# Two-block kernel: router work placed between projection matmuls, rows gathered in transposed halves, expert and feed-forward matmuls reordered

## The chip, the cores and the metric

One core of one Trainium2 chip runs the whole program, one launch. The metric is the device time in microseconds; the kernel before was timed three times, 1625.5, 1627.11 and 1628.01 us, median 1627.11.

## What is computed

256 tokens of 1024 values pass a first block and then a second. In the first block a norm, a projection, attention of the stick-breaking kind and a recurrent state mixer are followed by an output projection that is added to the stream. Then comes the mixture of experts that the change touches:

```python
xn = rmsnorm(h)
grp_prob = softmax(xn @ w_grp + b_grp);  g_idx = top-1 of 4 groups
sel = (xn @ w_exp + b_exp) of the 8 experts of that group;  top-2 of softmax(sel)
combine = group value * expert value / sum of the two expert values
for e in range(32):
    y = y + combine[:, e:e+1] * ((silu(xn @ w_gate[e]) * (xn @ w_up[e])) @ w_down[e])
h = rmsnorm(h + y) * final_norm_g
```

An expert is 1024 to 256 and back to 1024. The second block has two layers of feed-forward (1024 to 2816 and back), a mixer, and feed-forward again; each feed-forward is `x + 0.5 * (silu(x @ w_gate) * (x @ w_up)) @ w_down`.

## The kernel before

**Words.** P is 128, the tokens are two tiles of 128 (j = 0, 1), the 1024 columns two halves (n = 0, 1) of 512. `K.mx` is a PSUM pool of two buffers of two banks, `K.acc` one of four buffers of one bank. Weights of the second block are split into a high part wh (ScalarE, line 277) and a rest wl (VectorE, line 258), and the stream likewise, so that a product takes three matmuls. Most small operations go through wrappers (class InOrder, its call on line 48) that keep the order of the program on their engine; the profile gives them all line 48. What is not written with the wrappers (`K.ordered = False` with `nc.tensor`, line 246) may be reordered by the framework's scheduler.

**Front's end** (from `out_sb`, about lines 907 to 954). The output projection runs over eight weight units f; its last four (f = 4 to 7, list `us`) are held for both token tiles. With `K.ordered` set, the first tile's projection is finished and added to x, its factor is computed, then the second tile's projection runs: column half 0 over four units, the first tile's transposes (`turn`, `turned`), column half 1, then the first tile's router logits.

**Moe.run.** 96 loads of 1 MB (gate, up and down of 32 experts, in quads q of four: 4 gate, 4 up, 4 down) go on SP's queue into 22 ring slots. The slots alias tiles of the front, so that a load waits until the front's last reader of that place is done; the 16th load (gate of expert 7) lies on held output-projection weights, the next ones on the first tile's transposed rows and further weights. From the 23rd load on (`load_next(4)`, three times a quad) a load waits for the matmuls that read the slot's last content. Of the last load (down of expert 31) the two column halves are issued as two transfers.

At its start the second tile is added, transposed and given its logits; `select(j)` (twelve VectorE steps) picks group and experts of a tile, a product with a triangular matrix ranks the tokens of an expert, and one-hot matrices `OH[j]` of 32 slots an expert come out of it. `weave` alternates the steps of two such lists. `with_x(j, n)` starts the accumulators `py[j, n]` with x itself. Then, for each quad:

- `up(q, 0)`, `up(q, 1)`: gate and up of the quad's 4 x 32 slot rows, four experts side by side on TensorE (tile 128*32);
- `gather(q+1, j)`: the next quad's rows, one-hot times x; copied to SBUF by ScalarE and VectorE (`gathered`), transposed with a column step of 8, scaled and copied (`rows_T`, tiles XG0 and XG1);
- `act`: Silu on ScalarE, a product on VectorE, two transposes, a copy to hT;
- `down`: hT times the four experts' down weights, for n = 0 and then n = 1;
- `back(q, y, n)`: y is split into yh (ScalarE) and yl (VectorE) and added to `py[j, n]` through the transposed one-hot.

In quad 0 the slot weights and the rest of the `with_x` come in too. `all_tokens` is a branch for experts with more than 32 tokens.

**The tail** (from `V, S = K.V, K.S`). For each j and n: `square` (ScalarE, sum of squares of py), `gained` (VectorE, py times a gain into x) and `square_x` (ScalarE, squares of that). Their order is written out by hand, with quad 7's second `back` between. From the sums `e0` (twelve small VectorE steps) makes the factor of the second block's first norm, and `xn` is the first tile that TensorE transposes for the second block.

**Feed-forward** (from line 1728, `for i in range(1, FF // 256)`). For each column block i four accumulators (gate and up, two halves b each) collect over four weight units. X is stored as high part and rest side by side, so a wh matmul has 512 columns and a wl matmul 256. In a unit all eight wh matmuls of the four accumulators come first, then all eight wl matmuls. Blocks with even i use the mx pool, with odd i the acc pool; the down stage ("dn") uses 512 columns throughout.

## Time and profile before

| what | value |
|---|---|
| median of three runs | 1627.11 us |
| profiled execution: its own time | 1625.12 us |
| profiled execution: span of the core | 1623.4 us |
| granted clock, mean | 0.981 |
| PE busy | 1549.9 us, 95% of the span |
| DVE, ACT busy | 64%, 51% |
| moved by DMA | 331 MB, mean 204 GB/s |

The profile shows one execution. Times of its rows count from the start of the span; the engines are PE (TensorE), PEld (its weight loads), DVE (VectorE), ACT (ScalarE), POOL (GpSimd) and SP (the engine whose queue issues the loads). A timeline row is `start, length, engine, line, operation, out<-in, shape, xcount`, and in brackets the idle time of the engine ahead of it and what ended that; equal instructions in a row are one row. The ends of matmuls are modelled and overlap their successors: the pitch of matmuls is read from starts. PSUM tiles all bear the name of their pool (mx, acc).

### The profile page before, as it was taken

What the parts mean: (1) busy time and instruction counts of PE and PEld (TensorE: products, weight loads), DVE (VectorE), ACT (ScalarE), POOL (GpSimd) and SP (SyncE); (2) the same over time, 40 slices, a digit from 0 to 9 for tenths busy, and PEclk for the clock granted to TensorE, in tenths of its full rate; (3) what the DMA queues carried; (4) which work ended last, traced back from release to release, by engine and by line L of the source; (5) the groups of instructions that cost most, each with busy time, mean ns of one, the idle gap of its engine ahead of it and who ended that gap; (6) DMA issues with size and microseconds to landing.
All of it is one profiled execution on the core that took longest, in us unless ns stands there. A gap on an engine that the chain in (4) does not pass through costs nothing.

```text
span 1623.4 us, 25106 instructions
## 1 busy us (share of the span) xinstructions
PE 1549.9 (95%) x9734; PEld 1283.6 (79%) x9734; DVE 1036.6 (64%) x1916; ACT 828.3 (51%) x1408; POOL 43.5 (3%) x134
## 2 busy tenths in 40 slices
PE   7999998887799999999999999999999999999998
PEld 6989874343378888889878888888888989778887
DVE  7866551111377656868986665666648779876653
ACT  6633421111356544668645554456546687455643
POOL 4000000000100000000000000000000000000000
PEclk9999998999999999999999999999999999999999
DMA  6431599999956555553456665656566434556653
GB/s 209 136 102 66 202 369 388 421 420 420 374 182 194 182 194 176 181 163 104 156 182 195 185 196 183 202 182 185 176 203 203 157 118 151 173 157 188 197 178 111
DMA packets 195644, 331.29 MB, mean 204 GB/s; under 512 B 11972, under 2 KB 150674, under 8 KB 183362
## 3 DMA queue, kind: packets, MB, share of 16 engines
q1 hardware_dynamic: 186208, 315.19, 56.4%
q0 software_dynamic: 4528, 13.41, 2.5%
q8 instruction: 77, 1.26, 0.3%
q10 hardware_dynamic: 4786, 1.05, 0.3%
q14 instruction: 45, 0.37, 0.1%
HBM read 328.25 MB, written 1.38 MB: 203 GB/s over the span
## 4 chain that ended last, share of the span: by engine, by line
PE 70%; DMA 6%; DVE 4%; ACT 2%; issue 1%; SPq 0%; ACTq 0%; DVEq 0%
PE acc L246 39%; PE mx L246 19%; PE acc L48 7%; PE mx L48 4%; DMA mw<-in_exp_w_down 2%; DMA mw<-in_exp_w_up 1%; DMA mw<-in_exp_w_gate 1%; DVE wl L258 1%; DVE wl L48 1%; PE mx L1969 0%; DMA wr<-in_w_in 0%; ACT wh L277 0%; PE mx L1993 0%; DMA wr<-in_ffn_w_up 0%; DVE ul L258 0%
## 5 line engine op out<-in xcount | busy, mean ns | idle before, releaser
L258 DVE TENSOR_TENSOR wl<-wr,wh 128x1024 fp32r<-128x1024 f32 x358 | 436.7, 1224 | 269.8 <-ACT wh L277 267.3
L277 ACT ACTIVATE wh<-wr 128x1024 fp32r<-128x1024 f32 x358 | 377.9, 1058 | 363.3 <-PE acc L246 249.5
L246 PE MATMUL acc<-X,wh 128*128 128x256 f32 (+1 forms) x1664 | 357.1, 329 | 0.0
L246 PEld LDWEIGHTS acc<-X,wh 128*128 128x128 f32 x1664 | 277.2, 191 | 25.4 <-issue 4.2
L246 PE MATMUL acc<-X,wl 128*128 128x256 f32 x1152 | 237.2, 284 | 0.0
L246 PEld LDWEIGHTS acc<-X,wl 128*128 128x128 f32 x1152 | 186.3, 191 | 6.9
L246 PE MATMUL mx<-X,wh 128*128 128x512 f32 x640 | 161.9, 393 | 0.0
L246 PEld LDWEIGHTS mx<-X,wh 128*128 128x128 f32 x640 | 114.5, 189 | 19.9
L246 PE MATMUL acc<-wh,hh 128*128 128x512 f32 x288 | 112.1, 389 | 0.0
L246 PE MATMUL acc<-wl,hh 128*128 128x512 f32 x288 | 112.1, 389 | 0.0
L246 PE MATMUL acc<-wh,hl 128*128 128x512 f32 x288 | 112.0, 389 | 0.0
L246 PEld LDWEIGHTS mx<-X,wl 128*128 128x128 f32 x640 | 88.3, 190 | 7.0
L246 PE MATMUL mx<-X,wl 128*128 128x256 f32 x640 | 90.5, 282 | 0.0
L48 PE MATMUL mx<-mw,XG 128*32 128x256 f32 x1024 | 64.6, 396 | 9.3 <-DMA mw<-in_exp_w_up 5.9
L48 PEld LDWEIGHTS mx<-mw,XG 128*32 128x32 f32 x1024 | 34.2, 114 | 37.9 <-issue 9.2
L246 PEld LDWEIGHTS acc<-wh,hl 128*128 128x128 f32 x288 | 54.1, 188 | 11.3
L246 PEld LDWEIGHTS acc<-wh,hh 128*128 128x128 f32 x288 | 54.1, 188 | 11.2
L246 PEld LDWEIGHTS acc<-wl,hh 128*128 128x128 f32 x288 | 54.1, 188 | 11.0
L246 PE MATMUL acc<-wh,m 128*128 128x512 f32 x192 | 61.4, 394 | 0.0
L48 DVE COPY xr<-mx 128x512 f32<-128x512 f32 x8 | 5.5, 691 | 74.1 <-ACT xr L48 74.1
L246 PE MATMUL acc<-xh,wh 128*128 128x256 f32 x176 | 50.3, 286 | 0.0
L246 PE MATMUL acc<-xh,wl 128*128 128x256 f32 x176 | 49.9, 283 | 0.0
(641 smaller groups left out, 2537.4 us busy)
## 6 DMA issues: line engine op xcount, KB each, us to landing
wr<-in_w_in SPq DMA_DIRECT2D x44, 1024.0 KB, 5.4
wr<-in_ffn_w_gate SPq DMA_DIRECT2D x88, 512.0 KB, 4.0
wr<-in_ffn_w_up SPq DMA_DIRECT2D x88, 512.0 KB, 5.1
wr<-in_ffn_w_down SPq DMA_DIRECT2D x40, 1024.0 KB, 5.0
mw<-in_exp_w_gate SPq DMA_DIRECT2D x32, 1024.0 KB, 14.8
mw<-in_exp_w_up SPq DMA_DIRECT2D x32, 1024.0 KB, 16.7
mw<-in_exp_w_down SPq DMA_DIRECT2D x31, 1024.0 KB, 17.6
wr<-in_w_out SPq DMA_DIRECT2D x20, 1024.0 KB, 5.0
```

Of the source, the lines that this page charges most:

```text
L48: return lambda *a, **k: self.tc.keep_in_program_order(f(*a, **k))
L246: self.engines()[2].matmul(out, l, r, start=start, stop=stop, skip_group_check=share)
L258: i = self.K.engines()[0].tensor_sub(l, v, h)
L277: self.K.engines()[1].activation(h, v[:, q:q + c], AF.Copy)
```

## The change

The order of the front's end: half of the second tile's projection is moved behind the first tile's transposes, and the first tile's logits, the second tile's first add and its first transposes ahead of the last units. `gather` reads x with a column step of 8, so that the gathered rows come out in the order in which the transposes want them; copying and transposing go by halves with tiles of their own (xr0, xr1). The start of Moe.run runs the first tile's selection ahead of the second tile's logits, and the second tile's selection in one piece between the two gathers. In a quad the activation's first two steps go ahead of the next gather, and the first half's result is copied while the second half's matmuls run. In quad 7 the second half is split: experts 28 to 30 with the others, expert 31 behind the first half's `back` and the squares. The tail's squares are in a new order. In the feed-forward units each accumulator gets its two wh and then its two wl matmuls before the next accumulator's turn.

```diff
@@ -940,18 +940,24 @@
             out_mm(u, f, 0, n, False, True)
             router.add(x, 0, n, acs[0, n], acs[0, n])
         run(router.factor(0))
-        for n in range(2):
-            if n:
-                for h in range(2):
-                    router.turn(x, 0, h)
-                for h in range(2):
-                    router.turned(0, h, xT[h])
-            for f, u in us:
+
+        def last(n, fu):
+            for f, u in fu:
                 out_mm(u, f, 1, n, False, f == 7)
-        for n in range(2):
-            router.logits(0, n, xT[n])
+        last(0, us[:2])
+        for h in range(2):
+            router.turn(x, 0, h)
+        for h in range(2):
+            router.turned(0, h, xT[h])
+        last(0, us[2:])
+        last(1, us[:2])
+        for h in range(2):
+            router.logits(0, h, xT[h])
+        router.rest = [acs[1, n] for n in range(2)]
+        router.add(x, 1, 0, acs[1, 0], acs[1, 0])
+        router.turn(x, 1, 0)
+        last(1, us[2:])
         K.ordered = False
-        router.rest = [acs[1, n] for n in range(2)]
 
 
 NRING = 22
@@ -1113,34 +1119,40 @@
             return [lambda: K.V.tensor_add(rank[:, j], negm[:, j], pr[:, j]), lambda: place(j, 0, 4)]
 
 
-        XG, pg, xr = [None, None], [None], [None]
+        XG, pg, xr = [None, None], [None], [None, None]
 
         def gather(q, j):
 
             if j == 0:
-                pg[0] = K.mx.tile([P, 2, 512], F32, name="mx")
+                pg[0] = K.mx.tile([P, 2, 4, P], F32, name="mx")
             for n in range(2):
-                K.mm(pg[0][:, n], OH[j][:, 4 * q:4 * q + 4].rearrange("p e c -> p (e c)"), x[:, j, n * 512:(n + 1) * 512],
-                     j == 0, j == 1, share=True)
-
-        def gathered():
-            xr[0] = wk.tile([P, 2, 512], F32, name="xr")
+                K.mm(pg[0][:, n], OH[j][:, 4 * q:4 * q + 4].rearrange("p e c -> p (e c)"),
+                     x[:, j].rearrange("p (f k) -> p k f", k=KD)[:, 4 * n:4 * n + 4], j == 0, j == 1, share=True)
+
+        def gathered(n):
             V, S, _ = K.engines()
-            S.activation(xr[0][:, 0], pg[0][:, 0], AF.Copy)
-            V.tensor_copy(xr[0][:, 1], pg[0][:, 1])
-
-        def rows_T():
-
-            pt = K.mx.tile([P, KD, P], F32, name="mx")
-            r = xr[0].rearrange("p n f -> p (n f)")
+            xr[n] = wk.tile([P, 4, P], F32, name=f"xr{n}")
+            if n:
+                V.tensor_copy(xr[n], pg[0][:, n])
+            else:
+                S.activation(xr[n], pg[0][:, n], AF.Copy)
+
+        pt_ = [None]
+
+        def rows_T(n):
+
+            if n == 0:
+                pt_[0] = K.mx.tile([P, KD, P], F32, name="mx")
+            pt = pt_[0][:, 4 * n:4 * n + 4]
             V, S, T_ = K.engines()
-            for k in range(KD):
-                T_.transpose(pt[:, k], r[:, k::KD], K.ident)
-            for b in range(2):
-                XG[b] = wk.tile([P, 4, P], F32, name=f"XG{b}")
-            V.tensor_mul(XG[0], pt[:, 0:4], gp[:, 0:4, None].to_broadcast([P, 4, P]))
             for k in range(4):
-                S.activation(XG[1][:, k], pt[:, 4 + k], AF.Copy, scale=gp[:, 4 + k:5 + k])
+                T_.transpose(pt[:, k], xr[n][:, k], K.ident)
+            XG[n] = wk.tile([P, 4, P], F32, name=f"XG{n}")
+            if n == 0:
+                V.tensor_mul(XG[0], pt, gp[:, 0:4, None].to_broadcast([P, 4, P]))
+            else:
+                for k in range(4):
+                    S.activation(XG[1][:, k], pt[:, k], AF.Copy, scale=gp[:, 4 + k:5 + k])
         OHT = [None]
 
         def slots_T(q):
@@ -1222,7 +1234,7 @@
                         for j in range(2):
                             K.mm(a[j][:, 0:512], xT[j][k // 4][:, k % 4], g, k == 0, k == KD - 1)
                     for j in range(2):
-                        hT = self.act(wk, a[j], ce[:, j], self.r[j])
+                        _, hT = self.act(wk, a[j], ce[:, j], self.r[j])
                         for n in range(2):
                             for k in range(2):
                                 d = piece(wd[bass.ds(e, 1)].rearrange("o (p k) f -> p (o k) f", k=2)[:, k, n * 512:(n + 1) * 512])
@@ -1236,16 +1248,11 @@
                     K.mm(a[32 * i:32 * i + 32, 256 * hf:256 * hf + 256], XG[k // 4][:, k % 4, 32 * i:32 * i + 32],
                          W["gu", 4 * q + i, hf][:, k], k + hf == 0, k == KD - 1, share=True)
 
-        def down(q, hT):
-            ys = []
-            for n in range(2):
-                y = K.mx.tile([P, 512], F32, name="mx")
-                for k in range(2):
-                    for i in range(4):
-                        K.mm(y[32 * i:32 * i + 32], hT[:, k, 32 * i:32 * i + 32],
-                             W["d", 4 * q + i, 0][:, k, n * 512:(n + 1) * 512], k == 0, k == 1, share=True)
-                ys.append(y)
-            return ys
+        def down_mm(q, hT, y, n, experts):
+            for k in range(2):
+                for i in experts:
+                    K.mm(y[n][32 * i:32 * i + 32], hT[:, k, 32 * i:32 * i + 32],
+                         W["d", 4 * q + i, 0][:, k, n * 512:(n + 1) * 512], k == 0, k == 1, share=True)
 
         def spare(name, slot, dt=F32):
 
@@ -1258,61 +1265,61 @@
             py[j, n] = K.acc.tile([P, 512], F32, name="acc")
             K.mm(py[j, n], K.ident, x[:, j, n * 512:(n + 1) * 512], True, False)
 
-        def back(q, ys, n):
+        yp = {}
+
+        def out_rows(q, y, n):
+
             if q == 7 and n:
                 t = spare("yr", 12, F32R)
-                yh, yl = t[:, 0:512], t[:, 512:1024]
+                yp[n] = t[:, 0:512], t[:, 512:1024]
             else:
-                yh, yl = [wk.tile([P, 512], F32R, name=t) for t in ("yh", "yl")]
-            K.engines()[1].activation(yh, ys[n], AF.Copy)
-            K.engines()[0].tensor_sub(yl, ys[n], yh)
-            for y in (yh, yl):
-                for j in range(2):
-                    K.mm(py[j, n], OHT[0][:, q % 2, j * P:(j + 1) * P], y, False, q == 7 and y is yl)
+                yp[n] = [wk.tile([P, 512], F32R, name=t) for t in ("yh", "yl")]
+            V, S, _ = K.engines()
+            S.activation(yp[n][0], y[n], AF.Copy)
+            V.tensor_sub(yp[n][1], y[n], yp[n][0])
+
+        def back(q, n):
+            yh, yl = yp[n]
+            for j, y in [(0, yh), (0, yl), (1, yh), (1, yl)] if q == 7 else [(0, yh), (1, yh), (0, yl), (1, yl)]:
+                K.mm(py[j, n], OHT[0][:, q % 2, j * P:(j + 1) * P], y, False, q == 7 and y is yl)
 
         K.ordered = True
         xT = [wk.tile([P, 4, P], F32, name="xTm", tag=t) for t in ("XG1", "yh")]
         OH[0] = K.xp.tile([P, NE, CAP], F32, name="OH0", tag="grow")
         OH[1] = (B.c if B else wk).tile([P, NE, CAP], F32, name="OH1", tag="big")
         s0, s1 = select(0), select(1)
-        for n in range(2):
-            self.add(x, 1, n, self.rest[n], self.rest[n])
-        for n in range(2):
-            self.turn(x, 1, n)
-            self.turned(1, n, xT[n])
-        for n in range(2):
-            self.logits(1, n, xT[n])
+        run(s0[:8])
+        self.turned(1, 0, xT[0])
+        self.logits(1, 0, xT[0])
+        self.add(x, 1, 1, self.rest[1], self.rest[1])
+        self.turn(x, 1, 1)
+        self.turned(1, 1, xT[1])
+        run(s0[8:])
         f1 = self.factor(1)
-        run(f1[:4])
-        weave(f1[4:], s0[:6])
-        for n in range(2):
-            with_x(0, n)
-        weave(s0[6:], s1[:6])
         K.mm(pr[:, 0], lt, mask[:, 0])
         K.mm(pr[:, 1], K.ones, mask[:, 0], stop=False, share=True)
-        with_x(1, 0)
-        run(s1[6:8])
-        weave(s1[8:10], ranks(0))
-        run(s1[10:])
+        run(f1[:3])
+        weave(f1[3:5], ranks(0))
+        run(f1[5:])
+        self.logits(1, 1, xT[1])
+        with_x(0, 0)
+        gather(0, 0)
+        run(s1)
         K.mm(pr[:, 1], lt, mask[:, 1], start=False, share=True)
-        gather(0, 0)
         run(ranks(1))
         gather(0, 1)
-        gathered()
-        rows_T()
+        for n in range(2):
+            gathered(n)
+            rows_T(n)
         for j in range(2):
             place(j, 4, NE)
-
-        def rows(q):
-            for j in range(2):
-                gather(q, j)
-            gathered()
 
         for q in range(NE // 4):
             if q == 2:
                 all_tokens(nmax)
             if q == 2:
-                rows_T()
+                for n in range(2):
+                    rows_T(n)
             a = K.mx.tile([P, 1024], F32, name="mx")
             up(a, q, 0)
             load_next(4)
@@ -1327,24 +1334,40 @@
                 slot_weights(0, 1)
             if q % 2 == 0:
                 slots_T(q)
-            if q != 7:
-                rows(q + 1)
             if q == 6 and B:
                 par = B.params(Carve(K.xp.tile([P, D], F32, name="par", tag="grow")))
                 next(par)
-            hT = self.act(wk, a, ws[:, q:q + 1], ws[:, 8 + q:9 + q])
-            if q not in (1, 7):
-                rows_T()
+            act = self.act(wk, a, ws[:, q:q + 1], ws[:, 8 + q:9 + q])
+            next(act)
+            if q != 7:
+                gather(q + 1, 0)
+            hT = next(act)
+            if q != 7:
+                gather(q + 1, 1)
+                for n in range(2):
+                    gathered(n)
+            if q == 0:
+                with_x(0, 1)
+                with_x(1, 0)
             if q == 7 and B:
                 next(par, None)
-            y = down(q, hT)
+            y = [K.mx.tile([P, 512], F32, name="mx") for _ in range(2)]
+            down_mm(q, hT, y, 0, range(4))
+            out_rows(q, y, 0)
+
+            down_mm(q, hT, y, 1, range(3 if q == 7 else 4))
             load_next(4)
+            if q not in (1, 7):
+                for n in range(2):
+                    rows_T(n)
+            back(q, 0)
             if q == 0:
                 slot_weights(1, 8)
                 nmax = beyond()
                 with_x(1, 1)
-            for n in range(1 if q == 7 else 2):
-                back(q, y, n)
+            if q != 7:
+                out_rows(q, y, 1)
+                back(q, 1)
 
         K.ordered = False
 
@@ -1376,19 +1399,19 @@
         def gained(j, n):
             V.tensor_mul(x[:, j, half[n]], py[j, n], fg[:, half[n]])
 
-        gained(0, 0)
-        back(7, y, 1)
-        square(1, 0)
-        square(0, 0)
-        gained(1, 0)
-        gained(0, 1)
-        square_x(0, 0)
-        square(0, 1)
-        gained(1, 1)
-        square_x(0, 1)
-        square(1, 1)
-        square_x(1, 0)
-        square_x(1, 1)
+        for j in range(2):
+            square(j, 0)
+            gained(j, 0)
+            square_x(j, 0)
+        K.ordered = True
+        down_mm(7, hT, y, 1, [3])
+        out_rows(7, y, 1)
+        back(7, 1)
+        K.ordered = False
+        for j in range(2):
+            square(j, 1)
+            gained(j, 1)
+            square_x(j, 1)
         run(e0)
         steps, ra = K.rsqrt_steps(K.sm, a1, [P, 2], 1.0, 0.0, "fr", True)
         return [f[1] for f in fs], ra, e1, steps
@@ -1400,10 +1423,11 @@
         V, S, T_ = K.engines()
         S.activation(sg, a[:, 0:256], AF.Silu, scale=r)
         V.scalar_tensor_tensor(sg, a[:, 256:512], w, sg, op0=OP.mult, op1=OP.mult)
+        yield
         for k in range(2):
             T_.transpose(a[:, 512 + k * P:512 + (k + 1) * P], sg[:, k::2], K.ident)
         S.activation(hT, a[:, 512:768].rearrange("p (k t) -> p k t", k=2), AF.Copy)
-        return hT
+        yield hT
 
 
 NZ, NXBC, NDT = 0, 1024, 2560
@@ -1728,13 +1752,13 @@
         for i in range(1, FF // 256):
             ac = sums(i)
             for wh, wl, k0, m in self.units(("gu", i), 0, KD):
-                bs = [(ac[b][s], slice(s * 256 + b * P, s * 256 + (b + 1) * P)) for b in range(2) for s in range(2)]
-                for a, c in bs:
-                    for k in range(m):
-                        K.mm(a, wh[:, k, c], X[:, k0 + k], k0 + k == 0, False, share=True)
-                for a, c in bs:
-                    for k in range(m):
-                        K.mm(a[:, 0], wl[:, k, c], X[:, k0 + k, 0], False, k0 + k == KD - 1, share=True)
+                for b in range(2):
+                    for s in range(2):
+                        a, c = ac[b][s], slice(s * 256 + b * P, s * 256 + (b + 1) * P)
+                        for k in range(m):
+                            K.mm(a, wh[:, k, c], X[:, k0 + k], k0 + k == 0, False, share=True)
+                        for k in range(m):
+                            K.mm(a[:, 0], wl[:, k, c], X[:, k0 + k, 0], False, k0 + k == KD - 1, share=True)
             if i == 1:
                 pt = K.mx.tile([P, 2, T], F32, name="mx")
                 for j in range(2):
```

## Rows read from the trace of the kernel before

**Rows 1.** The page's 40 equal slices (40.6 us each): the DMA share.
```profile
DMA  6431599999956555553456665656566434556653
```

**Rows 2.** Windows: length, busy PE, PEld, DVE, ACT, POOL, clock, DMA share, GB/s.
```profile
222.00:230.00 8.00, 7.75 (x55) 6.36 (x53) 4.85 (x31) 1.95 (x6) 0.00 (x0) 1.00 0.89 331
242.00:250.00 8.00, 7.31 (x83) 4.03 (x72) 0.77 (x5) 0.60 (x1) 0.00 (x0) 1.00 0.87 324
272.00:280.00 8.00, 8.00 (x124) 4.28 (x117) 0.00 (x0) 0.00 (x0) 0.00 (x0) 1.00 0.82 312
340.00:350.00 10.00, 9.31 (x137) 5.16 (x136) 0.00 (x0) 0.60 (x1) 0.00 (x0) 1.00 1.02 419
470.00:620.00 150.00, 150.00 (x806) 129.77 (x805) 95.85 (x139) 81.81 (x140) 0.00 (x0) 1.00 0.59 190
```

**Rows 3.** Chain of waits, middle of the expert stage: start, us, what.
```profile
333.51 19.82 DMA mw<-in_exp_w_gate
```

**Rows 4.** Timeline of SP's queue: the sixteenth load's issue.
```profile
222.50 0.33 SPq L1046 DMA_DIRECT2D mw<-in_exp_w_gate  x1
```

**Rows 5.** Timeline of TensorE, head of the expert stage: start, us, what.
```profile
222.98 1.87 PE L48 MATMUL acc<-wrt,xT 128*128 128x36 f32 x16
224.68 1.07 PE L48 MATMUL mx<-ident,x 128*128 128x128 f32 x8
231.35 3.68 PE L48 MATMUL mx<-x,OH 128*128 128x512 f32 x8
238.38 1.93 PE L48 MATMUL mx<-mw,XG 128*32 128x256 f32 x32 [0.79 <-DVE XG L48]
```

**Rows 6.** Tile views of xr and x by form: ns min/median/max.
```profile
L48 PEld LDWEIGHTS mx<-ident,xr x64: 186/193/230, 236.4 to 407.4; 128*128 128x128 f32 x64
L48 PEld LDWEIGHTS mx<-ident,x x16: 138/140/225, 219.1 to 225.4; 128*128 128x128 f32 x16
L48 PE MATMUL mx<-x,OH x24: 592/592/697, 231.3 to 281.5; 128*128 128x512 f32 x24
```

**Rows 7.** Timeline of TensorE, quad 0.
```profile
247.22 3.70 PE L48 MATMUL mx<-x,OH 128*128 128x512 f32 x8 [0.69 <-ACT OHT L1153]
253.97 0.54 PE L48 MATMUL mx<-ident,msg 128*128 128x128 f32 x2 [3.06 <-DVE msg L48]
```

**Rows 8.** Timelines of TensorE, ScalarE and VectorE, tail of the expert stage.
```profile
436.65 3.62 PE L48 MATMUL mx<-mw,mhT 128*32 128x512 f32 x26 [0.32 <-DMA mw<-in_exp_w_down]
440.31 0.60 ACT L1267 ACTIVATE yr<-mx 128x512 fp32r<-128x512 f32 x1 [1.06 <-PE mx L48]
442.32 0.60 ACT L48 ACTIVATE fsq<-acc 128x512 f32<-128x512 f32 x1 [0.21 <-DVE x L48]
441.55 2.49 DVE L48 TENSOR_TENSOR x<-acc,fg 128x512 f32<-128x512 f32 x4
447.06 1.42 DVE L48 SCALAR_TENSOR_TENSOR xn<-x,nri,grow 128x512 f32<-128x512 f32 x2 [0.45 <-ACT fsq L48]
```

**Rows 9.** Timeline of TensorE, feed-forward unit (single slots cut out) and down stage.
```profile
501.22 2.00 PE L246 MATMUL mx<-X,wh 128*128 128x512 f32 x8
501.45 0.40 PE L246 MATMUL mx<-X,wh 128*128 128x512 f32 x1
501.69 0.39 PE L246 MATMUL mx<-X,wh 128*128 128x512 f32 x1
503.06 1.12 PE L246 MATMUL mx<-X,wl 128*128 128x256 f32 x8
503.17 0.52 PE L246 MATMUL mx<-X,wl 128*128 128x256 f32 x3
504.01 2.00 PE L246 MATMUL mx<-X,wh 128*128 128x512 f32 x8
628.12 0.39 PE L48 MATMUL acc<-wh,hl 128*128 128x512 f32 x1
629.02 0.39 PE L48 MATMUL acc<-wh,hh 128*128 128x512 f32 x1
```

## The prediction

> **What bounds the kernel now.** I first read the slices of the page, the DMA row above all [rows 1]: the DMA share is 9 in tenths in six slices, from 203 to 446 us, and 3 to 6 after them, so the expert stage is bound by its loads and the second block by something else. The windows [rows 2] say how exactly: between 340 and 350 us the share is 1.02 at 419 GB/s, that is, full, while three stretches are not: 222 to 230 us (0.89), 242 to 250 (0.87) and 272 to 280 (0.82). Against full they lose about 8 x 0.11 = 0.9, 8 x 0.13 = 1.0 and 8 x 0.18 = 1.4 us. Whatever the change does to the engines inside the expert stage, it can give back at most these 3.3 us, because after the last of them the chain of waits stands on loads, from the gate load at 333.51 that it waits 19.82 us for [rows 3] to the last down load. The stage behind it, from 436.65 us until the first matrix work of the second block, is a serial path in which DMA no longer counts. In the second block TensorE doesn't stop: between 470 and 620 us, a feed-forward stage, it is busy 150.00 of 150 [rows 2], and only the pitch of its matmuls can move the time there.
>
> So there are three accounts: holes in the load stream, the serial tail of the expert stage, and the pitch of the feed-forward units. I use 0.2% of the median, 3.25 us, as what a measurement of this kernel can tell from no change.
>
> **Account 1, the head and the holes.** The sixteenth load, gate of expert 7, is issued at 222.50 [rows 4]; its slot lies on the output-projection weights whose last reader is the second tile's projection. Before, that projection, with the first tile's eight transposes inside, is done when the logit matmuls start, 222.98 [rows 5]. Now its 24 matmuls have in between them also the sixteen logit matmuls (222.98 to 224.68, 1.7 us) and four transposes of the second tile (half of the eight at 224.68, 1.07 us, so some 0.6 with their wait) [rows 5]. The last reader, and with it the issue, moves 2.3 to 2.6 us later, to about 225.1. The next load follows on the same queue at once, so the hole that is there already swallows part: growth between 1.7 (all of the old 0.9 lay behind that one load) and 2.6 (none); I take 1.9.
>
> What is moved forward in return: the first tile's logits and selection are ready earlier, but the second tile's are not. Its factor (about twelve small VectorE steps of 0.2) ends near 229.6, its selection then runs alone, twelve steps or 2.4 us, mask product, rank and one-hot come near 233, and gather(0,1) takes half of the 3.68 us that eight records take [rows 5] and ends near 235, where it ended before. The half-by-half copies let the first experts' matmuls start up to a microsecond before 238.38 [rows 5]; behind the copies ScalarE and VectorE still take turns on one PSUM tile. I count this as nothing, bounds -1 and +1.
>
> A load stream that is 1.9 late meets slots that come free as early as before, so the second hole (1.0) closes, being a wait for slots and not for data. The third hole comes from quad 0, where the slots are freed only after eight gather records (from 247.22) and then 3.06 us in which TensorE waits for the activation [rows 7]. With the activation ahead of the gather this wait has cover, worth up to 3.06 us on TensorE against a hole of 1.4: it closes. The two with_x pairs moved into quad 0 cost 2 x 2 records (about 0.45 each, 1.8 us in all, from the eight gather records) and still leave over 1 us. Sum of the account: +1.9 - 1.0 - 1.4 = -0.5; bounds -3.3 (no growth, all closed) and +1.6 (2.6 - 1.0, third hole stays). Quads 1 to 6 cost nothing: their cover is the full stream of loads [rows 2, 3]; if it went, their order would be worth about 3 us each.
>
> **The strided gather.** The gather now reads x with a step of eight words as its moving operand. No row shows that for a moving operand. The nearest pair is the stationary load: with the step of eight words ("ident,xr", old code) it takes 193 ns for 128 columns, contiguous ("ident,x") 140 [rows 6]. So the step costs 53/128 = 0.41 ns a column there. The gather moves a column in 3.68 us / 8 / 512 = 0.9 ns, and a 128-column load that took 0.41 more would stay below that if it took no more than 0.5 contiguous. I take 0, bounds 0 and +0.41 ns x 512 = 0.21 us a record. The transposes behind it become contiguous, 8 x 53 ns beside the matmuls: nothing. The Trainium skill, "Advanced Engine Details and Errata", SBUF Cachelines, says that a read which touches a new 16-byte line each time pays; by that rule this step of 32 bytes would be slower, and rows 6 agree for a stationary load. What it would do here is the fourth rival.
>
> **Account 2, the tail.** Before, the last load's second half is there in time: 26 records run through from 436.65 to 440.27 after one wait of 0.32 [rows 8], and y of the second half is copied (yr) at 440.31. The change moves expert 3's second-half matmuls behind the first half's back product. Alone they have no three others beside them: four records of about 0.44 instead of a quarter of a group, 1.7 us. The three others still take as long as the four, so TensorE gets to the back product at 440.2 as before, passes it in 1.0, and ends the lone expert near 443.0. The worse part is a queue: yr now stands on ScalarE behind four squares, and two of these need the gained product of VectorE. ScalarE and VectorE readers of one PSUM tile took turns before (the second square waits for "DVE x", 442.32 [rows 8]). With 0.60 a square, 0.62 a gained product (2.49/4) [rows 8] and 0.63 for a square of x, each half tile is a chain of about 2.0; two of them from 441.1 end at 445.1. Then yr 0.6, yl 0.7, the back product 0.9 to 447.3, again two chains until the last gained product at about 450.4, then twelve factor steps, 2.2, because the program keeps them behind all products. xn starts near 452.6 against 447.06 [rows 8]: +5.5. Low bound: if readers do not take turns, yr comes at 443.7 and xn at 449.4, +2.3; at the very least +1.7, the lone expert. High +6. I take +5.5. TensorE waits for xn in either case, so all of it is on the path. The early squares gain nothing, since the last square decides.
>
> **Account 3, the feed-forward units.** A unit now alternates two wh (512 columns) and two wl (256) four times instead of running eight and eight. A unit takes 2.79: 1.84 for wh (501.22 to 503.06) and 0.95 for wl (503.06 to 504.01) [rows 9]. The matrix work is the same; only the pitch where the kinds change can differ. Within a unit, the change from wh to wl is followed by one slot of 0.11 (503.06 to 503.17) where the other seven share 0.84, 0.12 each [rows 9]: a gain of 0.01 a change. The change back, at a unit's border, is followed by a slot of 0.24 (501.45 to 501.69) where the plain pitch of 512 columns is 0.225 (628.12 to 629.02, four slots) [rows 9]: a loss of 0.015 a change, if it is the change and not the border, where new weights come in. There are 160 units (four feed-forward layers, ten column blocks, four units each), and three more changes of each kind in a unit. Gain alone: 480 x 0.01 = -4.8. Gain and loss: 480 x 0.005 = +2.4. If also all wh slots fell to 0.2267 as in the down stage, 8 x 0.0033 x 160 = another -4.3, -9.1. I take -4.8, because the gain is seen inside a unit where nothing but the kind changes, and the loss only at a border; bounds -9.1 and +2.4. That the order is kept is not sure either: this part is not in the strict program order.
>
> **Sum.** -0.5 + 0 + 5.5 - 4.8 = +0.2 on the profiled execution's 1625.12 (span 1623.4 and 1.7 around it). That execution is 2.0 under the median of three, 1627.11, on whose scale I give the forecast: 1627.3.
>
> **The rivals.**
> *The pitch does not fall* (the sign turns here). Mechanism: a matmul's slot is its columns plus a fixed share, whatever stands before it, and a slot of 0.11 is only paid back by one of 0.24. For it: both stand beside the same change in rows 9. Against it: the border. Account 3 is then 0 to +2.4 and the time 1632 to 1634.5. It decides from an account 3 above -1.8, where the sum passes +3.25 slower. The same comes out if the order of the units is not kept.
> *The pitch falls further*, wh too: 1627.3 - 4.3 = 1623.0. For it: a 512-column slot of 0.225 exists in the down stage; against it: that stage has no 256-column matmul that would load weights in a hurry.
> *Readers of one PSUM tile run side by side*, or yr slips ahead: tail +2.3, 1627.3 - 3.2 = 1624.1. Against it: row 442.32 and the wait named in it [rows 8].
> *The strided gather is slow*: 0.21 a record; gather(0,1) and its transposes 0.9 later, quad 0 1.7 longer. Then the second hole stays and the third closes only in part: account 1 about +2.2, time 1630.0. By the skill's rule named above this would be the case. Against it: the moving operand is read slower than the strided stationary one.
>
> **How the numbers follow.** Forecast 0.40 (its own range 1624.3 to 1630.3), no fall of pitch 0.30, further fall 0.15, readers side by side 0.10, slow gather 0.05. Low end: further fall and a better account 1 (-1.5) give 1621.5; high end: 1634.5 and half a microsecond from account 1. So 1621 to 1635. Faster: two thirds of the further fall, a half of readers side by side, a fifth of the forecast's spread after rounding, 0.25. Slower: most of the first rival and half of the slow gather, 0.31. Same: 0.44.
>
> **What the new profile would show.** Right: the sixteenth load's issue near 225, DMA share near 1.0 in 242 to 250 and 272 to 280; gather records still at 592 ns; first xn of the second block 5 to 6 us further behind the last load's landing; units of 2.76. Wrong: units at 2.79 or above (first rival), wh slots of 0.225 throughout (second), yr ahead of the squares of x or squares beside gained products (third), gather records near 800 ns (fourth). If the last load lands more than 3 us earlier than before, my bound on the holes is wrong.

## The result and the profile after

The changed kernel is slower: median 1639.84 us of five runs (1634.82 to 1641.59) against 1627.11 for the kernel before in the same comparison (five runs, 1625.5 to 1629.01); ratio 1.0073, 95% interval 1.0056 to 1.0089. The span of the profiled execution is 1638.2 us, 14.8 above before. The forecast was 1627.3, range 1621 to 1635.

Where the time went is seen at one instant. The first xn of the second block, 447.06 before [rows 8], starts at 461.68, 14.6 later; from there to the end both kernels take the same (1623.4 - 447.06 = 1176.3, and 1638.2 - 461.68 = 1176.5). So everything is lost up to the end of the expert stage's tail. This stretch behind xn varies from 1173.4 to 1177.7 over the profiles of all kernels here, and its mean is 1176.0 with the new feed-forward order and 1175.8 with the old, so that order neither gains nor loses. Of the 14.6, 2.0 lie ahead of all that the change touches: TensorE's last transposes of the front ("ident,go", right before the second tile's projection) begin at 214.82 before and at 216.79 after (timelines of TensorE, before and after):

```profile
214.82 0.60 PE L48 MATMUL mx<-ident,go 128*128 128x128 f32 x4
```

```profile
216.79 0.60 PE L48 MATMUL mx<-ident,go 128*128 128x128 f32 x4
```

In the profiles of all kernels of this study these transposes begin between 212.28 and 217.78, so the front varies from execution to execution, and distances from them are the fairer measure. From there to xn it is 232.2 before and 244.9 after, 12.7 more, near the 11.9 of the ratio (0.73% of 1627.11). 6.2 of that lie up to the last run of down matmuls (221.8, to 436.65 [rows 8]; 228.1, to 444.86), that is in the head and the quads, and 6.4 in the tail.

The tile views of xr and OH (ns min/median/max) give the cause of the first part. The transposes' weight loads fall from 193 to 140 ns, as forecast, but a gather matmul takes 1098 instead of 592 [rows 6]:

```profile
L48 PEld LDWEIGHTS mx<-ident,xr x64: 138/140/230, 241.3 to 424.3; 128*128 128x128 f32 x64
L48 PE MATMUL mx<-x,OH x64: 1076/1098/1163, 232.1 to 418.0; 128*128 128x512 f32 x64
```

The timeline of TensorE through the head and quad 0 (start, us, what) shows it in place. Four gather records take 3.83 where eight took 3.68 [rows 5], the first experts' matmuls start 28.1 us behind the transposes of go (244.84) instead of 23.6 (238.38 [rows 5]), and in quad 0 the transposes of msg at 259.75, which waited 3.06 for the activation before [rows 7], wait no more:

```profile
232.12 3.83 PE L48 MATMUL mx<-x,OH 128*128 128x512 f32 x4
236.71 3.92 PE L48 MATMUL mx<-x,OH 128*128 128x512 f32 x4 [0.60 <-DVE OH L48]
244.84 9.45 PE L48 MATMUL mx<-mw,XG 128*32 128x256 f32 x128
256.01 3.92 PE L48 MATMUL mx<-x,OH 128*128 128x512 f32 x4 [0.69 <-ACT OHT L1165]
259.75 0.40 PE L48 MATMUL mx<-ident,msg 128*128 128x128 f32 x2
259.99 3.83 PE L48 MATMUL mx<-x,OH 128*128 128x512 f32 x4
```

That wait is closed by the new order, which sets the activation ahead of the gather and half of the gather ahead of these transposes, and not by the slow gather: with the new order and a fast gather it is 0.32 (e6), and with a slow gather in the old order all 15.0 us of such waits stay (e4).

The windows (length, busy PE, PEld, DVE, ACT, POOL, clock, DMA share, GB/s) show what that does to the loads. The three stretches that had shares of 0.89, 0.87 and 0.82 [rows 2] have become worse and more: 0.70, then 0.45, then 0.84 and 0.76. Against full these four lose 2.4 + 4.4 + 1.9 + 2.4 = 11.1 us, 7.8 more than before. The granted clock is 0.52, near the lower level of 1.2 GHz, in 242 to 250, right behind the waits for xr and XG that end the head; it was 1.00 there before [rows 2]. It fell a little later then: over 230 to 290 the mean is 0.89 in both kernels, so the clock does not make the difference. The windows after:

```profile
222.00:230.00 8.00, 7.26 (x50) 6.23 (x48) 4.70 (x22) 2.59 (x7) 0.00 (x0) 1.00 0.70 278
242.00:250.00 8.00, 6.62 (x58) 3.21 (x61) 4.96 (x15) 1.48 (x7) 0.00 (x0) 0.52 0.45 187
250.00:262.00 12.00, 11.31 (x97) 4.81 (x90) 0.86 (x4) 2.74 (x4) 0.00 (x0) 1.00 0.84 335
280.00:290.00 10.00, 10.00 (x133) 4.47 (x133) 0.48 (x1) 0.47 (x1) 0.00 (x0) 0.98 0.76 295
```

The sixteenth load is issued at 226.68 (SP's queue), 9.9 us behind the transposes of go instead of 7.7 (222.50 [rows 4]):

```profile
226.68 0.33 SPq L1052 DMA_DIRECT2D mw<-in_exp_w_gate  x1
```

The holes are the trace of the delay and not its whole cause. From the transposes of go to the last run of down matmuls TensorE is busy 20.1 us longer (185.1 before, 205.2 after) and idle 13.8 less (36.7 and 22.9): together the 6.2. Its groups by line and tile (busy us, mean ns, then idle time before them and what ended it) show where. Before:

```profile
L48 PE MATMUL mx<-mw,XG 128*32 128x256 f32 x1024 | 64.6, 396 | 9.3 <-DMA mw<-in_exp_w_up 5.9 <-issue 2.6 <-DVE XG L48 0.8
L48 PE MATMUL mx<-mw,mhT 128*32 128x512 f32 x256 | 36.7, 668 | 3.2 <-DMA mw<-in_exp_w_down 1.8 <-ACT mhT L48 0.9 <-ACT XG L48 0.2
L48 PE MATMUL mx<-x,OH 128*128 128x512 f32 x64 | 29.6, 605 | 2.7 <-ACT OHT L1153 2.7
L48 PE MATMUL mx<-ident,xr 128*128 128x128 f32 x64 | 9.5, 296 | 2.0 <-DVE xr L48 1.4 <-PEq L1202 0.6
L48 PE MATMUL mx<-ident,msg 128*128 128x128 f32 x16 | 4.1, 337 | 15.0 <-DVE msg L48 15.0
```

After:

```profile
L48 PE MATMUL mx<-mw,XG 128*32 128x256 f32 x1024 | 63.1, 400 | 1.4 <-issue 1.4
L48 PE MATMUL mx<-x,OH 128*128 128x512 f32 x64 | 62.0, 1103 | 3.4 <-ACT OHT L1165 2.7 <-DVE OH L48 0.6
L48 PE MATMUL mx<-mw,mhT 128*32 128x512 f32 x256 | 31.0, 595 | 0.5 <-ACT mhT L48 0.5
L48 PE MATMUL mx<-ident,xr 128*128 128x128 f32 x64 | 11.4, 304 | 8.2 <-DVE XG L48 5.5 <-DVE xr L48 1.4 <-ACT xr L48 0.7
L48 PE MATMUL mx<-ident,msg 128*128 128x128 f32 x16 | 3.3, 288 | 1.1 <-DVE msg L48 1.1
```

The gather takes 62.0 - 29.6 = 32.4 us more. Against it stands cover that it uses up. Of the 15.0 us in which TensorE waited for the activation (msg), 1.1 are left; the new order opens this room. The groups of up and down matmuls, busy and idle together, fall from 113.8 to 96.0, by 17.8: 10.6 of that is idle time, most of it waits for loads, the rest shorter busy time, of which no run shows how much is due to the loads. The transposes of the rows give 8.1 back (1.9 longer, 6.2 more waiting). That is 32.4 - 15.0 - 17.8 + 8.1 = 7.7 against the 6.2 measured. The busy times of groups overlap, and over all groups the same sum is 10.5, so such an account is good to some four microseconds only. No load is named any more among the releasers of these groups: the stage that was bound by loads is bound by TensorE, and of the chain of work that ended last DMA has 1% instead of 6% of the span (pages of the profile).

In the tail (timelines of TensorE, ScalarE, VectorE) the two squares and the gained products of the first halves take turns (449.29, 450.01, 450.74, and again), yr comes at 453.57, though expert 31's lone matmuls had ended at about 451.5, and its back product follows at 454.20:

```profile
444.86 3.63 PE L48 MATMUL mx<-mw,mhT 128*32 128x512 f32 x28 [0.47 <-ACT mhT L48]
449.65 1.90 PE L48 MATMUL mx<-mw,mhT 128*32 128x512 f32 x4
454.20 2.37 PE L48 MATMUL acc<-yr,OHT 128*128 128x512 f32 x4 [2.64 <-ACT yr L48]
449.29 0.60 ACT L48 ACTIVATE fsq<-acc 128x512 f32<-128x512 f32 x1 [1.32 <-PE acc L48]
450.74 0.63 ACT L48 ACTIVATE fsq<-x 128x512 f32<-128x512 f32 x1 [0.76 <-DVE x L48]
451.49 0.60 ACT L48 ACTIVATE fsq<-acc 128x512 f32<-128x512 f32 x1
453.57 0.58 ACT L48 ACTIVATE yr<-mx 128x512 fp32r<-128x512 f32 x1
450.01 0.69 DVE L48 TENSOR_TENSOR x<-acc,fg 128x512 f32<-128x512 f32 x1 [1.31 <-ACT fsq L48]
461.68 0.75 DVE L48 SCALAR_TENSOR_TENSOR xn<-x,nri,grow 128x512 f32<-128x512 f32 x1 [0.15 <-DVE nri L48]
```

In the feed-forward units the order of the program is kept, two and two. A pair of wl takes 0.23 (479.97 to 480.20), a pair of wh 0.47 (480.20 to 480.67), and four of each 2.79 (479.97 to 482.76), what a unit took before [rows 9]:

```profile
479.97 0.40 PE L246 MATMUL acc<-X,wl 128*128 128x256 f32 x2
480.20 0.63 PE L246 MATMUL acc<-X,wh 128*128 128x512 f32 x2
480.67 0.39 PE L246 MATMUL acc<-X,wl 128*128 128x256 f32 x2
482.76 0.40 PE L246 MATMUL acc<-X,wl 128*128 128x256 f32 x2
```

### The profile page after: what moved, and what is told of

Read it like the earlier page. It is cut to its first block, busy times and chain, and to the rows that moved or that the text cites. A ratio compares the mean times of both kernels' runs of the same rounds, so it can differ in the third digit from the quotient of the medians.

```text
span 1638.2 us, 24970 instructions
## 1 busy us (share of the span) xinstructions
PE 1575.3 (96%) x9734; PEld 1281.4 (78%) x9734; DVE 1040.3 (64%) x1916; ACT 836.5 (51%) x1408; POOL 43.5 (3%) x134
## 4 chain that ended last, share of the span: by engine, by line
PE 73%; DVE 4%; ACT 2%; DMA 1%; issue 1%; SPq 0%; POOL 0%; ACTq 0%; DVEq 0%
PE acc L246 38%; PE mx L246 18%; PE acc L48 8%; PE mx L48 8%; DVE wl L258 1%; DMA wr<-in_ffn_w_gate 1%; DVE wl L48 1%; DMA cr<-csd 0%; PE mx L1993 0%; ACT wh L277 0%; PE mx L2017 0%; ACT XG L48 0%; DMA wr<-in_ffn_w_up 0%; DVE XG L48 0%; ACT p L2008 0%
## 5 line engine op out<-in xcount | busy, mean ns | idle before, releaser
L246 PE MATMUL acc<-X,wh 128*128 128x256 f32 (+1 forms) x1664 | 396.9, 330 | 0.0
L246 PE MATMUL acc<-X,wl 128*128 128x256 f32 x1152 | 273.0, 282 | 0.0
L246 PEld LDWEIGHTS acc<-X,wh 128*128 128x128 f32 x1664 | 260.5, 191 | 5.3 <-issue 4.2
L246 PEld LDWEIGHTS acc<-X,wl 128*128 128x128 f32 x1152 | 218.6, 190 | 28.6
L246 PE MATMUL mx<-X,wh 128*128 128x512 f32 x640 | 201.6, 396 | 0.0
L246 PEld LDWEIGHTS mx<-X,wl 128*128 128x128 f32 x640 | 120.2, 188 | 28.4
L246 PE MATMUL mx<-X,wl 128*128 128x256 f32 x640 | 125.8, 278 | 0.0
L246 PEld LDWEIGHTS mx<-X,wh 128*128 128x128 f32 x640 | 97.4, 189 | 0.2
L48 PE MATMUL mx<-x,OH 128*128 128x512 f32 x64 | 62.0, 1103 | 3.4 <-ACT OHT L1165 2.7
L246 PEld LDWEIGHTS acc<-wh,hh 128*128 128x128 f32 x288 | 54.1, 188 | 11.1
L246 PEld LDWEIGHTS acc<-wl,hh 128*128 128x128 f32 x288 | 54.1, 188 | 11.1
## 6 DMA issues: line engine op xcount, KB each, us to landing
mw<-in_exp_w_gate SPq DMA_DIRECT2D x32, 1024.0 KB, 14.8
```

The costliest lines, as they stand in the source:

```text
L48: return lambda *a, **k: self.tc.keep_in_program_order(f(*a, **k))
L246: self.engines()[2].matmul(out, l, r, start=start, stop=stop, skip_group_check=share)
```

## The experiments

Each comparison has its own runs of the kernel before, on the same chip; ratios are to those. Their medians differ between the comparisons (1622.83 to 1627.11), so kernels of different comparisons are set against each other by their ratios. The changed kernel ran five times, e4 six times, e7 and e8 once, the others twelve times. "Go to xn" is the distance in the profile from the front's last transposes to xn, 232.2 us before, 244.9 in the changed kernel. "Chain" is its last part, from the start of the last long run of down matmuls, 10.4 us before (436.65 to 447.06).

| kernel | ratio to before, 95% interval | go to xn against before, us |
|---|---|---|
| changed kernel | 1.0073 [1.0056, 1.0089] | +12.7 |
| e1 contiguous gather in it | 1.0021 [1.0008, 1.0033] | +6.2 |
| e2 old tail in it | 1.0040 [1.0026, 1.0054] | +8.2 |
| e3 both | 0.9996 [0.9983, 1.0009] | -0.6 |
| e4 step of eight alone | 1.0115 [1.0093, 1.0137] | +18.5 |
| e5 feed-forward order alone | 1.0006 [0.9992, 1.0019] | -0.8 |
| e6 quads' order alone | 0.9982 [0.9967, 0.9998] | -2.3 |
| e9 e6 with yr behind squares | 1.0018 [1.0003, 1.0032] | +5.0 |
| e10 e6 with expert 31 split off | 0.9993 [0.9979, 1.0008] | -1.0 |
| e11 new head alone | 0.9991 [0.9975, 1.0006] | -2.0 |
| e12 e6 with another scratch slot | 0.9983 [0.9968, 0.9999] | -1.9 |

The -0.8 of e5, which changes nothing ahead of xn, shows how far a single such distance can be trusted.

**e1, contiguous gather in the changed kernel.**

```diff
-    K.mm(pg[0][:, n], OH..., x[:, j].rearrange("p (f k) -> p k f", k=KD)[:, 4 * n:4 * n + 4], ...)
+    K.mm(pg[0][:, n], OH..., x[:, j, n * 512:(n + 1) * 512], ...)
-    T_.transpose(pt[:, k], xr[n][:, k], K.ident)
+    T_.transpose(pt[:, k], xr[0].rearrange("p n f -> p (n f)")[:, 4 * n + k::KD], K.ident)
```

> The changed kernel, with the gather reading x in contiguous halves again (both halves copied before the transposes, which read with the step of eight). Theory S (the step of eight words makes a gather matmul 0.92 us instead of 0.43, which delays the first two quads and opens the load stream's holes from 3.3 to about 11 us): gather records back at 592 ns, the first experts' matmuls 3 to 5 us earlier, the holes back near 4, time 8 us under the changed kernel, 1630 to 1633. Rival H (the new order of the head alone opens the holes, whatever a gather takes): no less than 1637.

Ratio 1.0021 (median 1629.26 against 1625.02). The gather records are back at 592 ns, and the first experts' matmuls start 24.3 behind go instead of 28.1:

```profile
L48 PE MATMUL mx<-x,OH x64: 592/592/697, 232.5 to 407.4; 128*128 128x512 f32 x64
```

Against the changed kernel's 1.0073 the step of eight costs 0.52%, 8.5 us. Theory S; rival H falls.

**e2, the old tail in the changed kernel.** The edit takes the tail's lines from the kernel before.

```diff
-            down_mm(q, hT, y, 1, range(3 if q == 7 else 4))
+            down_mm(q, hT, y, 1, range(4))
...
-        for j in range(2):
-            square(j, 0)
-            gained(j, 0)
-            square_x(j, 0)
+        gained(0, 0)
+        out_rows(7, y, 1)
+        back(7, 1)
+        square(1, 0)
+        square(0, 0)
...
```

> The changed kernel with the tail of the kernel before (expert 31's second half with the others, yr ahead of the squares, squares and gained products in the old order). Theory S with a tail that costs by itself: from the last down matmuls to xn 10.4 us instead of 16.8, time 6.4 under the changed kernel, 1633 to 1634.5. Rival (the tail only looks long, since TensorE is late there anyway): 1638 to 1640.

Ratio 1.0040 (1631.68); chain 10.5 us (447.51 to 457.98). The tail costs 0.33%, 5.4 us by the times (4.1 by the pair e1 and e3), 6.4 by the chains of the profiles.

**e3, both edits.**

> Both edits together: what is left of the change is the order of the head, the activation ahead of the gather, and the feed-forward order. Theory S plus tail: both savings add, 1639.8 - 8 - 6.4 = 1625 to 1626, no slower than the kernel before. Rival H: 1631 or more. If the order of the head and of the quads gives back the holes that were there before, down to 1623.5.

Ratio 0.9996 (1625.53). From e1 to e3 the old tail gains 0.25%, 4.1 us. The two savings add up to the whole loss; what is left of the change is worth nothing that can be measured. With the old tail the step of eight costs 0.44%, 7.2 us (e2 against e3). In its profile the share is 0.78 in 220 to 230 us, where the late sixteenth load lies, and 0.98 in 240 to 250 and in 270 to 280.

**e4, the step of eight in the kernel before.**

```diff
-    K.mm(pg[0][:, n], OH..., x[:, j, n * 512:(n + 1) * 512], ...)
+    K.mm(pg[0][:, n], OH..., x[:, j].rearrange("p (f k) -> p k f", k=8)[:, 4 * n:4 * n + 4], ...)
```

> The kernel before, with the gather reading x with a step of eight words, so that the transposes read contiguous rows; nothing else. Theory S: gather records near 1080 to 1100 ns, first experts' matmuls 3.5 to 4 us later, quad 0's second gather 4 us longer, holes 3.3 + 4 to 8, time 1631 to 1635. Rival H: gather records may be slow but quads are under the loads: 1627.

Ratio 1.0115 (1643.96), more than either theory gave, and more than the whole change. The groups, and the last run of down matmuls on the timeline:

```profile
L48 PE MATMUL mx<-mw,XG 128*32 128x256 f32 x1024 | 61.3, 393 | 3.3 <-issue 2.5 <-DVE XG L48 0.8
L48 PE MATMUL mx<-x,OH 128*128 128x512 f32 x64 | 60.7, 1105 | 2.7 <-ACT OHT L1153 2.7
```

```profile
455.35 3.64 PE L48 MATMUL mx<-mw,mhT 128*32 128x512 f32 x32 [0.47 <-ACT mhT L48]
```

The gather takes 31.1 more, the waits for loads give 14.1 back (113.8 - 99.7 with the mhT group's 33.9 + 1.2), the waits for the activation stay at 15.0, the transposes take 1.0 more: 18.0, and the last run starts 18.4 later (455.35, transposes of go at 215.10). The expectation had counted only the head and quad 0, as the prediction had: all eight gathers pay, and the loads cover some 14 to 18 us in all. The same slow gather that costs 8.5 us in the changed kernel costs about 19 here: in the old order the 15.0 us of waits for the activation stay in full beside it, in the new one the gather fills them.

**e5, the feed-forward order alone.** The kernel before with that hunk.

> The kernel before with the feed-forward order of the change alone. Theory Z (a slot is its columns plus a fixed share, the order inside a unit moves nothing, as the pairs of 0.23 and 0.46 in the changed kernel's trace add up to 2.78 to 2.79 a unit): ratio within 0.1% of 1. Theory of the prediction (0.03 us a unit saved, 4.8 us): ratio 0.997.

Ratio 1.0006 (1623.55 against 1622.83). Theory Z; the forecast saving of 0.3% is outside the interval.

**e6, the quads' order alone**, contiguous gather, all else as before.

```diff
-            if q != 7:
-                rows(q + 1)
...
-            hT = self.act(wk, a, ws[:, q:q + 1], ws[:, 8 + q:9 + q])
+            next(act)
+            if q != 7:
+                gather(q + 1, 0)
+            hT = next(act)
+            if q != 7:
+                gather(q + 1, 1)
...
```

> The kernel before with the quads' order of the change alone (activation ahead of the gather, first half's rows copied beside the second half's matmuls, transposes behind the down matmuls), contiguous gather, old head, old tail, old feed-forward. Theory Q (the third hole, 1.4 us at 272 to 280, comes from TensorE's wait for the activation in quad 0, and the new head of the change gives that away again with the late sixteenth load): the share at 270 to 280 goes to 0.98 or more, the sixteenth load stays at 222 to 223, xn 1 to 1.5 us earlier, ratio 0.9990 to 0.9995, too little to be told from no change by the time alone. Rival (the old hole only moves to a later quad): xn where it was.

Ratio 0.9982 (1619.26 against 1622.83), more than the theory gave: the one part of the change whose gain is outside its interval, though barely (upper end 0.9998); e12, which has the same order, repeats it. TensorE's wait for msg in quad 0 is 0.32 instead of 3.06 [rows 7], over all quads 1.4 instead of 15.0, and the third hole is closed (timeline and group of TensorE, windows). Other waits take up most of what is saved (for loads 12.3 instead of 7.7 us, ahead of the rows' transposes 8.3 instead of 2.0), so that from go to xn 2.3 us come out. Which part of the new order does it was not tried apart.

```profile
247.47 0.50 PE L48 MATMUL mx<-ident,msg 128*128 128x128 f32 x2 [0.32 <-DVE msg L48]
L48 PE MATMUL mx<-ident,msg 128*128 128x128 f32 x16 | 3.4, 291 | 1.4 <-DVE msg L48 1.4
```

```profile
242.00:250.00 8.00, 6.99 (x50) 3.23 (x46) 0.86 (x4) 2.96 (x5) 0.00 (x0) 1.00 0.96 368
272.00:280.00 8.00, 8.00 (x55) 2.76 (x47) 1.87 (x3) 2.05 (x4) 0.00 (x0) 1.00 1.01 420
```

**e7 and e8, steps of four and of two words**, one execution each, the transposes with a step of two and of four.

```diff
+    x[:, j].rearrange("p (f k) -> p k f", k=4)[:, 2 * n:2 * n + 2]      (e7)
+    x[:, j].rearrange("p (f k) -> p k f", k=2)[:, n:n + 1]              (e8)
```

> The kernel before, the gather reading x with a step of four words (16 bytes), the transposes with a step of two. Theory L (what counts is whether each read comes to a new line of 16 bytes): gather records 1098 ns as with a step of eight, transposes' weight loads 140. Rival P (the price grows with the step): records between 592 and 1098, near 800.

> The kernel before, the gather reading x with a step of two words (8 bytes), the transposes with a step of four. Theory L: gather records 592 ns as contiguous, transposes' weight loads 193 (each column on a line of its own). Rival P: records near 700, weight loads between 140 and 193. Rival A (any step but one is slow): records 1098, weight loads 193.

The tile views, e7 first:

```profile
L48 PE MATMUL mx<-x,OH x64: 1077/1078/1147, 234.3 to 432.0; 128*128 128x512 f32 x64
L48 PEld LDWEIGHTS mx<-ident,xr x64: 195/214/231, 242.5 to 436.7; 128*128 128x128 f32 x64
```

```profile
L48 PE MATMUL mx<-x,OH x64: 609/611/717, 230.6 to 400.8; 128*128 128x512 f32 x64
L48 PEld LDWEIGHTS mx<-ident,xr x64: 195/210/231, 235.2 to 404.8; 128*128 128x128 f32 x64
```

The gather with a step of four words takes 1078 ns, about what eight take, with two words 611, about what one takes: so the price comes between 8 and 16 bytes, as theory L says, and does not grow from 16 to 32. The times go with it: 1648.36 and 1623.35, beside a median of 1622.83, and go to xn is 20.2 longer in e7 and 0.3 in e8. The two patterns differ in one thing more: a record of e7 reads two stretches of 256 columns, one of e8 a single stretch of 512. No run separates this from the step. The weight loads fit no theory: 214 ns with a step of two, 210 with four.

**e9 and e10, the tail taken apart** (both on e6). In e9 the squares of the first halves go ahead of yr, and expert 31 is not split off; in e10 expert 31 is split off, and yr and the squares keep the old order.

```diff
+        for j in range(2):                                              (e9)
+            square(j, 0)
+            gained(j, 0)
+            square_x(j, 0)
+        out_rows(7, y, 1)
...
+            down_mm(q, hT, y, 1, range(3 if q == 7 else 4))             (e10)
...
+        down_mm(7, hT, y, 1, [3])
         gained(0, 0)
         out_rows(7, y, 1)
...
```

> The kernel of e6, with the squares and gained products of the first halves ahead of yr as in the change, but expert 31's second half computed with the others. Theory Y (the cost of the new tail is yr's place on ScalarE behind four squares in turns with the gained products; expert 31's lone matmuls are hidden under them): from the start of the last run of down matmuls to xn 16 to 16.8 us, against 10.4 in e6. Rival (prediction's sum: both cost): 14.5 to 15.

> The kernel of e6, with expert 31's second half behind the first half's back product, but yr and the squares in the old order. Theory Y: the lone expert now stands on the path, 10.4 + 1.7 to 2 = 12.1 to 12.4 us from the last run of down matmuls to xn. Rival (it is a free filler in any order): 10.4 to 10.8.

e9: ratio 1.0018, 0.36% (5.9 us) above e6; chain 454.23 - 437.16 = 17.1, a little more than theory Y gave (TensorE, ScalarE, VectorE):

```profile
437.16 3.62 PE L48 MATMUL mx<-mw,mhT 128*32 128x512 f32 x26 [0.31 <-DMA mw<-in_exp_w_down]
445.98 0.58 ACT L48 ACTIVATE yr<-mx 128x512 fp32r<-128x512 f32 x1
454.23 1.41 DVE L48 SCALAR_TENSOR_TENSOR xn<-x,nri,grow 128x512 f32<-128x512 f32 x2 [0.16 <-DVE nri L48]
```

e10: ratio 0.9993; chain 446.32 - 434.29 = 12.0, with yr right behind the lone matmuls:

```profile
434.29 2.78 PE L48 MATMUL mx<-mw,mhT 128*32 128x512 f32 x22 [0.32 <-DMA mw<-in_exp_w_down]
438.33 1.90 PE L48 MATMUL mx<-mw,mhT 128*32 128x512 f32 x4
440.27 0.60 ACT L1274 ACTIVATE yr<-mx 128x512 fp32r<-128x512 f32 x1 [3.38 <-PE mx L48]
446.32 1.42 DVE L48 SCALAR_TENSOR_TENSOR xn<-x,nri,grow 128x512 f32<-128x512 f32 x2 [0.44 <-ACT fsq L48]
```

The new order of yr and the squares costs the whole 6.6 us by itself; the split costs 1.6 when nothing hides it, and in the changed kernel it is hidden under the queue. That is theory Y in the main, but yr's place is not all of it. yr starts 8.8 us behind the start of the run instead of 3.7, and from yr to xn it takes 8.3 instead of 6.8 [rows 8], so some 1.5 us lie behind yr. There the square, the gained product and the square of x of one half follow one another; in the old order the four gained products run through without a wait (441.55, 2.49 us [rows 8]), with a square of another half beside them. What either would cost alone was not tried.

**e11, the new head alone.**

```diff
+        last(0, us[:2])
...
+        last(1, us[2:])
...
+        run(s0[:8])
+        self.turned(1, 0, xT[0])
...
```

> The kernel before with the new head alone (front's end and start of the expert stage up to the first gather; contiguous gather, quads, tail, feed-forward as before). Theory Q (the new head delays the sixteenth load from 222.5 to about 225 to 227 and starts the first experts 1 to 1.5 us later, nothing comes back): share 220 to 230 from 0.92 to 0.78, the later holes partly closed, xn 0.5 to 2.5 us later, ratio 1.0003 to 1.0015. Rival (the earlier logits pay): first experts' matmuls earlier, ratio under 0.9995.

Ratio 0.9991 (1621.35 against 1623.65): no change that can be measured. The sixteenth load comes 9.9 us behind the transposes of go instead of 7.7, as theory Q says, and the share is 0.83 in 220 to 230; but the first experts start as early as before (23.7 behind go, 23.6 before), the share is 0.98 or more in every later ten us to 310, and xn is 2.0 earlier. Neither theory is proved by the time; by the profile theory Q's "nothing comes back" is wrong. With the quads' order the gain of the two doesn't add (e3).

**e12, e6 with the squares' scratch in another slot.**

```diff
-        sq = spare("fsq", 13)
+        sq = spare("fsq", 14)
```

> The kernel of e6 with the squares' scratch tile in another ring slot, so that xn of the second block does not lie on the memory that ScalarE's last square writes. Theory: the wait of 0.45 us ahead of xn goes, xn starts right behind the factor's last step; ratio to the kernel before 0.998 as e6, 0.0003 less at most. Rival (the wait is for x itself, read by the last square): the 0.45 stay.

Ratio 0.9983 (1620.92). xn waits for nothing any more, and the chain is 10.1:

```profile
432.92 3.62 PE L48 MATMUL mx<-mw,mhT 128*32 128x512 f32 x26 [0.32 <-DMA mw<-in_exp_w_down]
443.02 1.41 DVE L48 SCALAR_TENSOR_TENSOR xn<-x,nri,grow 128x512 f32<-128x512 f32 x2
```

e6 and e12 are the versions that beat both kernels, the old one by less than 0.2%; between them the times show no difference.

## Why the prediction was wrong, point by point

**The strided gather** is the step that failed: "I take 0, bounds 0 and +0.41 ns x 512 = 0.21 us a record". Measured by the groups' busy time it is 0.97 instead of 0.46 us, +0.5 a record, outside the bounds. The error was to carry the price of a stationary load over to a moving operand as a price per column that a slow reader can hide. The argument fails on its own rows: it holds "if it took no more than 0.5 contiguous", but rows 6 have 140 / 128 = 1.09 ns a column for the contiguous load and 193 / 128 = 1.51 for the strided one, both above the gather's 0.9. If a moving column took those 1.51, a record would take 0.77 us (an estimate), 0.3 more than before, so by these rows even the bound of 0.21 was too low. The rival "The strided gather is slow" was there, with a chance of 0.05 and 1630.0, at the same 0.21 a record. The Trainium skill, "Advanced Engine Details and Errata", SBUF Cachelines, was read against it and set aside with that argument; e7 and e8 show the moving operand doing what that section says.

**"Quads 1 to 6 cost nothing: their cover is the full stream of loads"** is the second step that failed: it left 48 of the 64 gather records, 24 of the 32 us, out of the sum. A full stream covers TensorE only as long as TensorE waits for it somewhere. In the groups of before the idle time ahead of the up and down matmuls is 12.5 us (9.3 and 3.2), 7.7 of it ended by a load, and the waits for the activation, which the new order turns into cover, are 15.0. Against that the change set 64 records x 0.5 = 32. With this sum over the stage the slow-gather rival would have stood at 32 - 15.0 - 12.5 = 4.5 over the forecast, near 1632 and not at 1630; this is an estimate made afterwards, and as rough as the account above.

**The tail** was right in its mechanism and nearly in its size: +5.5 forecast, chain +6.4 in the profile, 4.1 to 5.4 by the times (e1 to e3, e2). Most of the remaining 0.9 is that each of the four chains of square, gained product and square of x takes 2.2 instead of 2.0 (449.29 to 451.49). The lone expert's 1.7 was in the sum's path only as a low bound; e9, without the split, is no faster in its chain (17.1 against 16.8), so it costs nothing beside the queue.

**The feed-forward units**: "the gain is seen inside a unit where nothing but the kind changes, and the loss only at a border" chose wrongly between the two. The first rival was right: a slot of 0.11 is paid back by one of 0.24. e5 has 1.0006, +1.0 us with an interval of -1.3 to +3.1, against -4.8 forecast and 0 to +2.4 in the rival.

**The head and the holes**: the sixteenth load came 2.2 later by the distance from go, against 2.3 to 2.6 forecast, and the later holes close for it (e3, e11). That the first experts start as early as before holds too, without the step of eight (e11); with it they start 4.5 later, and the two head gathers take 4.1 longer (3.83 and 3.92 instead of 3.68 together). The activation's wait of 3.06 gave the third hole back as forecast (e6): 2.3 us from go to xn, 2.9 by the ratio, against 1.4. In the changed kernel nothing of this is seen, since the slow gather opens larger holes.

So the sum of 0.2 should have read: head and quads about 0 to -2, the gather +7 to +9, the tail +4 to +6, the units 0. The units alone would have left the time at 1632, inside the range; the gather takes it out.

## What to carry to other kernels

When a transposition is saved by reading with a stride, ask which operand takes the stride: here a matmul's moving operand kept its pace with a step of 8 bytes and ran at about half of it with 16 and 32, so that 32 us of TensorE time were added, 7 to 9 us of the kernel's time, to save 53 ns on the weight load of a transpose. Work put "under the loads" has a budget: add up the idle time ahead of the groups that wait, over the whole stage, and set the sum of the added work against it. A wait for another engine counts as cover only where the order lets the added work stand in it: the 15.0 us here were cover in the new order and none in the old. And an early start of work that is not late, as the squares here, is a cost when it stands in an in-order queue ahead of the work that is.

## What the runs showed of the hardware that was not expected

- The moving operand, fp32 with 512 columns: 592 ns contiguous, 611 with a step of 8 bytes, 1078 with 16, 1098 with 32. This agrees with the section of the Trainium skill named above, by which a line of 16 bytes wants two hits; the runs show the times and not the lines.
- The stationary operand of a transpose, 128 columns: 140 ns contiguous, 214 with a step of 8 bytes, 210 with 16, 193 with 32. It does not follow that rule: the step that costs the moving operand nothing is the dearest here. The step is not all that counts: the gather's own load of OH, contiguous, takes 190 ns (median, kernel before).
- ScalarE and VectorE took turns on one PSUM tile in the tails shown (449.29, 450.01, 450.74 in the changed kernel; the wait for "DVE x" at 442.32 before [rows 8]); whether the chip or the program's dependences make them do so was not tried.
